# The last feed-forward product of a transformer encoder layer, turned so that tokens lie on the partitions

## The chip, the cores and the metric

The kernel runs on one core of a Trainium2 chip. The metric is the device time in microseconds of one execution of the whole program. Times before: 2081.9, 2083.98 and 2084.88 us in three runs, median 2083.98.

## The reference

Two sequences (`x_prompt`, `x_sample`) of 512 tokens and 1024 channels go through one encoder layer, each by itself, in float32. Only the end matters here:

```python
def rms_norm(x, g):
    y = x * lax.rsqrt(jnp.mean(x * x, axis=-1, keepdims=True) + EPS)
    return y * g

def swiglu(x, w_gate, w_up, w_down):          # D_FF = 2816
    return (silu(x @ w_gate) * (x @ w_up)) @ w_down

# end of the layer, for each sequence:
x = x + 0.5 * swiglu(rms_norm(x, ffn2_norm), ffn2_w_gate, ffn2_w_up, ffn2_w_down)
return rms_norm(x, final_norm)
```

Ahead of it lie a first feed-forward of the same form, attention and an mLSTM memory, which the change doesn't touch.

## The kernel before

Every float32 product is made from three passes: each operand is split into a high and a low part, and high x high, high x low and low x high are summed in PSUM.

**The second feed-forward's down product.** The two sequences and the two halves of the channels form a 2 x 2 block product, which is computed by the seven products of a Strassen scheme (named B11, B21, T2, T3, T4, T1, B22 in the order `DOWN`) and not by eight. `ffn_down` runs over 28 steps (`n_steps`): four chunks of the inner dimension (`CHUNKS`; the last is 8, 9, 10, three units each), and the seven products in each. In a step, `products` takes four blocks of 128 channels (`d`, `DH` = 4); in each block nine matmuls (three units, three passes) multiply 128x128 weights by 512 tokens into one PSUM bank: channels lie on the partitions, tokens along the row. Products T1 and B22 share a bank: B22 goes on accumulating where T1 stopped. Banks come from pools: `MM` (3 buffers, tile `mm`), `PO` (1, `pso`), `PS` (2, `pss`), `PT` (2, `pst`).

`flush_` (L597) evicts each bank on VectorE as `acc = 0.5 * psum + acc` into `xs[0]`, `xs[1]`, `e16` or `e5`. `xs[s]` holds sequence s of the layer's output with channels on the partitions: slots 0 to 3 the lower 512 channels, 4 to 7 the upper. In the last chunk it calls `done` as parts are final: sequence 0 after B21 (lower) and T4 (upper), the upper half of sequence 1 after T1, its lower half after B22, the very last step. That last step runs in two halves of 256 tokens (`halves`), so its matmuls have 256 columns.

**The final norm.** The sum over channels is needed for each token, and the output has tokens on its rows, so the results are turned by TensorE: `turn_out` (L1407) transposes four 128x128 blocks, one group of 128 tokens by 512 channels, into one `PS` or `PT` bank.

- `finish0` (sequence 0): sums of squares were collected in `acc0` during the flushes; `col_sums` (L200) transposes and reduces them, `stats` and `rsqrt_cols` (L165) compute 1/rms by an integer trick and three Newton steps, all on VectorE; then eight times transposes, one VectorE pass (`put_out`, L1420: times 1/rms times `final_norm`) and one transfer.
- `finish1_upper` (after T1): transposes of the upper half of sequence 1, a square with a row sum on ScalarE (`square`, L1435), and a multiply by `final_norm` on VectorE (L1442).
- `finish1(th)` (after each half of the last step): transposes of the lower half for two groups of 128 tokens, squares with sums in two pieces, 1/rms for both groups by `rsqrt_cols` in columns, then for each group two passes and two transfers.

All output transfers are issued from the SP queue, in order.

**The order of the work.** Each engine runs its instructions in a fixed order. A planner sets it: every instruction has a priority, by its place in the program, and an engine takes the ready one of lowest number. `shifted(n)` adds n to the numbers of a block; `LATER` = 100, used for `finish0`, sets it back by 100 instructions. So transposes of `finish0` and `finish1_upper` stand among the matmuls of the last step.

Of the kernel before, what the change touches and what calls it, by code (L numbers as in the profile page):

```python
# [16 lines left out]
P = 128  # L17
S = 512
D = 1024
KD = D // P  # L20
DFF = 2816
NF = DFF // P
EPS = 1e-6
# [3 lines left out]
def encoder(ctx, tc, I, outs):  # L27
    nc = tc.nc
# [106 lines left out]
    def A(shape, dtype=F32, name="a"):  # L135
        return apool.tile(shape, dtype, tag="a", name=nm(name))

    xs = [None, None]

    def xhl_tiles():  # L140
        return A([P, KD, S], F32R, "xh"), A([P, KD, S], F32R, "xl")
# [54 lines left out]
    def stats(acc):  # L196

        return rstd_cols(col_sums(acc), 4, D)

    def col_sums(acc, bs=(0, 1, 2, 3)):  # L200
        p = PT()
        for b in bs:
            nc.tensor.transpose(p[:, b * P:(b + 1) * P], acc[:, b * P:(b + 1) * P], ident)
        c = spool.tile([P, len(bs)], F32, tag=f"cs{len(bs)}", bufs=4, name=nm("cs"))
        nc.vector.tensor_reduce(c, p[:, bs[0] * P:(bs[-1] + 1) * P].rearrange("p (b d) -> p b d", d=P), axis=AX.X,
                                op=ALU.add)
        return c
# [294 lines left out]
    DH = KD // 2  # L502
    n_steps = len(DOWN) * len(CHUNKS)

    def ffn_down(wd, rb, ring, tail, xres, done, at_step, hook, halves=None):
        n = n_steps
        rt = [A([P, 4, 2, S], F32R, "rt") for _ in range(3)]
        e16 = A([P, KD, S], F32, "e16")
        xs[0], xs[1] = A([P, KD, S], F32, "xs"), A([P, KD, S], F32, "xs")
        e5 = A([P, DH, S], F32, "e5")  # L510
        right = [[t[:, q] for q in range(3)] for t in rt] + [[t[:, 3] for t in rt]]
# [65 lines left out]
        def products(i, ts, ds=range(DH)):  # L577
            m = DOWN[i % 7]
            first = m in (B11, T2_, T1)
            grp = "Y" if m in (T2_, T3, T4) else "X"  # L580
            for d in ds:
                if first:
                    banks[grp, d] = (((PS, PS, PT, PT) if grp == "Y" else (MM, MM, MM, PO))[d])()
                p = banks[grp, d][:, ts]
                us = left[i]
                for q, u in enumerate(us):
                    r = right[(i + 3) % 4][q]
                    for k, (a, b) in enumerate(((0, 0), (0, 1), (1, 0))):
                        nc.tensor.matmul(p, u[:, a, d * P:(d + 1) * P], r[:, b, ts],  # L589
                                         start=(first and q == 0 and k == 0), stop=(q == len(us) - 1 and k == 2),  # L590
                                         skip_group_check=True)
                flush_(i, d, p, ts)

        def add(t, u):
            V_.tensor_tensor(t, t, u, op=ALU.add)

        def flush_(i, d, p, ts):  # L597
            m, last = DOWN[i % 7], i >= n - 7
            acc = {B11: e16[:, d], T2_: e16[:, DH + d], T1: e5[:, d], B21: xs[0][:, d], T4: xs[0][:, DH + d],
                   T3: xs[1][:, DH + d], B22: xs[1][:, d]}[m]  # L600
            if last and m == T1:
                acc = xs[1][:, DH + d]
            if i < 7 and m in (B11, T2_, T1):
                nc.scalar.activation(acc, p, AF.Copy, scale=0.5)
            else:
                V_.scalar_tensor_tensor(acc[:, ts], p, 0.5, acc[:, ts], op0=ALU.mult, op1=ALU.add)
            if not last:
                return
            if m == B11:
                add(xs[0][:, DH + d], acc)  # L610
                add(xs[1][:, DH + d], acc)
                add(xs[1][:, d], acc)
            elif m == T2_:
                add(xs[1][:, d], acc)
            elif m == B21:
                add(xs[1][:, DH + d], e5[:, d])
                done(0, d, None)
            elif m == T4:
                done(0, DH + d, None)
            elif m == T1:  # L620
                done(1, DH + d, None)
            elif m == B22 and ts.stop - ts.start == S:
                done(1, d, None)
            elif m == B22 and d == DH - 1:
                done(1, d, ts.start * 2 // S)

        refill()
        for i in range(4):
# [6 lines left out]
        sums(CHUNKS[0])  # L635
        tail()
        for i in range(n):
            if i == n - 1 and halves:
                products(i, slice(0, S // 2))
                products(i, slice(S // 2, S))  # L640
            else:
                products(i, whole)
            prep(i + 2)
            load_right(i + 4)
            if i == 1:
                free.extend((1, *h4[k:k + 2]) for k in (0, 2))
                refill()
            if i == at_step:
                hook()
# [15 lines left out]
    def small(w, tag):  # L665
        return spool.tile([P, w], F32, tag=tag, bufs=2 if tag != "asm" else 6, name=nm(tag))
# [740 lines left out]
    def turn_out(s, b, half, p, ks=range(4)):  # L1407
        for k in ks:
            nc.tensor.transpose(p[:, k * P:(k + 1) * P], xs[s][:, half * 4 + k, b * P:(b + 1) * P], ident)
        return p  # L1410

    def put_out(s, b, half, p, r):

        o = T2()
        if s and half and b == 0:
            V_.tensor_scalar(o, p, r, None, op0=ALU.mult)
        elif s and half:
            nc.scalar.activation(o, p, AF.Copy, scale=r)
        else:
            V_.scalar_tensor_tensor(o, p, r, fn[half], op0=ALU.mult, op1=ALU.mult)  # L1420
        nc.sync.dma_start(outs[s][0, b * P:(b + 1) * P, half * S:(half + 1) * S], o)
# [9 lines left out]
    upper = []  # L1431

    def square(i, b, p):
        w = p.shape[-1]
        nc.scalar.activation(T2(F32, "f2")[:, 0:w], p, AF.Square, scale=D ** -0.5, accum_out=sq1[:, i, b:b + 1])  # L1435

    def finish1_upper():
        for b in range(4):
            p = turn_out(1, b, 1, (PS, PT)[b % 2]())
            square(0, b, p)  # L1440
            t = T2()
            V_.tensor_tensor(t, p, fn[1], op=ALU.mult)  # L1442
            upper.append(t)

    def finish1(th):
        bs = slice(2 * th, 2 * th + 2)
        cut = 2 * P
        ps_ = PS(), PT()
        for ks in (0, 1), (2, 3):
            for i in range(2):  # L1450
                turn_out(1, 2 * th + i, 0, ps_[i], ks)
                if ks[0] == 0:
                    square(1, 2 * th + i, ps_[i][:, 0:cut])
        sm, a = small(2, "fs2"), small(2, "fs2")
        V_.scalar_tensor_tensor(sm, sq1[:, 0, bs], EPS, sq1[:, 1, bs], op0=ALU.add, op1=ALU.add)
        for i in range(2):
            square(2, 2 * th + i, ps_[i][:, cut:S])
        V_.tensor_tensor(a, sm, sq1[:, 2, bs], op=ALU.add)
        r = rsqrt_cols(a, 2)
        with shifted(0 if th else LATER):  # L1460
            for j in range(4):
                i, half = j % 2, 1 - j // 2
                b = 2 * th + i
                put_out(1, b, half, upper[b] if half else ps_[i], r[:, i:i + 1])

    def done2(s, d, th):
        if s == 0:
            acc0[0] = sq_add(xs[0][:, d, :], acc0[0], "R", eng=V_ if d >= DH else None)
            if d == KD - 1:
                with shifted(LATER):  # L1470
                    finish0()
        elif d == KD - 1:
            finish1_upper()
        elif th is not None:
            finish1(th)

    ffn_down(I["ffn2_w_down"][0], rbuf[1], up.ring, tail, x2buf, done2, n_steps - 7, load_fn, halves=True)


def host_consts():  # L1480
# [39 lines left out]
```

## Time and profile before

| | |
|---|---|
| median of three runs | 2083.98 us (2081.9 to 2084.88) |
| the profiled execution | 2082.11 us |
| its span | 2080.3 us |
| granted TensorE clock | 0.997 of full speed |
| instructions | 27215 |
| busy: PE, PEld, DVE, ACT, POOL | 99%, 81%, 75%, 43%, 5% of the span |
| DMA | 454.33 MB moved, mean 218 GB/s |

The span runs from the first to the last event of the profiled execution; 1.8 us lie around it. PE is TensorE's matmuls (transposes too), PEld its weight loads, which overlap them, DVE VectorE, ACT ScalarE, POOL GpSimd, SP the engine that issues most transfers. A row of the timeline has the start in us, the duration, the engine, the line of the kernel, the operation, the tile written and those read, the shapes, and in brackets how long the engine idled before it and for whom. A row of a group has a count, the busy time in us, the mean of one in ns, and the idle time before. The mean duration of a matmul contains its way through the array, which overlaps the next one: its cost to TensorE is the pitch in the chain.

### The profile page before, as it was taken

The numbers are of one execution on the slowest core, as the hardware profiler recorded it, in microseconds if no ns is written. First come the engines' busy times: TensorE is split into PE (matmuls) and PEld (weight loads), VectorE is DVE, ScalarE is ACT, GpSimd is POOL, SyncE is SP. The second block draws the span as 40 slices with busy tenths as digits, with TensorE's granted clock in tenths as the row PEclk, the third lists the DMA queues.
The fourth block names the chain that finished last, engine by engine and source line by source line (L and its number), as shares of the span: only waits on it lengthen the run. The fifth ranks groups of instructions, "written<-read, shape, count | busy, mean of one in ns | idle before, by whom it ended". The sixth has DMA issues, their size and how long they took to land.

```text
span 2080.3 us, 27215 instructions
## 1 busy us (share of the span) xinstructions
PE 2060.4 (99%) x9478; PEld 1691.4 (81%) x9478; DVE 1551.1 (75%) x2836; ACT 894.6 (43%) x1645; POOL 97.7 (5%) x114
## 2 busy tenths in 40 slices
PE   8999999999999999999999999999999999999998
PEld 6888888888888877888878788888888888888887
DVE  7888888786797897575567646555788888786797
ACT  6544444443234566463345443324444444442222
POOL 1000000001003000100120000002000000000000
PEclk9999999999999999999999999999999999999999
DMA  9655655599766655777684345677656555599753
GB/s 280 203 173 194 193 171 182 200 342 362 262 222 243 218 152 174 265 240 268 210 286 160 107 149 190 208 255 245 200 177 200 192 172 182 187 348 347 270 189 116
DMA packets 307065, 454.33 MB, mean 218 GB/s; under 512 B 20064, under 2 KB 178864, under 8 KB 305904
## 3 DMA queue, kind: packets, MB, share of 16 engines
q1 hardware_dynamic: 305056, 447.13, 63.6%
q0 software_dynamic: 1872, 5.46, 0.8%
q8 instruction: 75, 1.23, 0.2%
q14 instruction: 62, 0.51, 0.1%
HBM read 285.63 MB, written 166.89 MB: 218 GB/s over the span
## 4 chain that ended last, share of the span: by engine, by line
PE 95%; DVE 3%; DMA 1%; ACT 1%; issue 0%; SPq 0%; DVEq 0%; ACTq 0%
PE mm L755 20%; PE pss L333 17%; PE pst L333 11%; PE mm L333 10%; PE mm L589 9%; PE pst L589 4%; PE pss L589 4%; PE mm L739 4%; PE pso L589 3%; PE pso L1029 1%; PE pss L1002 1%; PE pso L739 1%; PE pst L1021 1%; PE pso L1165 1%; PE pst L755 1%; PE pss L755 1%
## 5 line engine op out<-in xcount | busy, mean ns | idle before, releaser
L755 PE MATMUL mm<-xh,w 128*128 128x512 f32 x896 | 290.4, 394 | 0.0
L333 PE MATMUL pss<-xc,w 128*128 128x512 f32 x1056 | 256.2, 391 | 0.6 <-DVE t L364 0.6
L333 PE MATMUL mm<-xc,w 128*128 128x512 f32 x1056 | 253.4, 391 | 2.0 <-DVE w L292 0.7
L333 PE MATMUL pst<-xc,w 128*128 128x512 f32 x1056 | 253.6, 389 | 0.0
L333 PEld LDWEIGHTS pss<-xc,w 128*128 128x128 f32 x1056 | 196.9, 188 | 47.8 <-DVE t L364 7.2
L333 PEld LDWEIGHTS mm<-xc,w 128*128 128x128 f32 x1056 | 197.3, 188 | 45.2 <-DVE w L292 1.4
L333 PEld LDWEIGHTS pst<-xc,w 128*128 128x128 f32 x1056 | 198.2, 188 | 41.2
L755 PEld LDWEIGHTS mm<-xh,w 128*128 128x128 f32 x896 | 167.7, 188 | 33.5
L589 PE MATMUL mm<-rt,w 128*128 128x512 f32 (+1 forms) x819 | 188.4, 384 | 0.0
L755 PE MATMUL mm<-xl,w 128*128 128x512 f32 x448 | 176.2, 393 | 0.0
L589 PEld LDWEIGHTS mm<-rt,w 128*128 128x128 f32 x819 | 151.3, 188 | 29.8
L291 ACT ACTIVATE w<-t 128x512 fp32r<-128x512 f32 x176 | 106.9, 627 | 139.0 <-issue 55.2
L292 DVE TENSOR_TENSOR w<-t,w 128x512 fp32r<-128x512 f32 x176 | 118.3, 689 | 54.9 <-ACT w L291 52.9
L333 PE MATMUL pss<-xc,f 128*128 128x512 f32 x528 | 126.8, 389 | 0.0
L333 PEld LDWEIGHTS pss<-xc,f 128*128 128x128 f32 x528 | 99.1, 188 | 20.6
L657 ACT ACTIVATE w<-wr 128x512 fp32r<-128x512 f32 x72 | 45.1, 632 | 138.2 <-PE pso L589 70.8
L657 ACT ACTIVATE w<-t 128x512 fp32r<-128x512 f32 x82 | 51.8, 632 | 107.4 <-PE pst L589 62.4
L755 PEld LDWEIGHTS mm<-xl,w 128*128 128x128 f32 x448 | 84.2, 188 | 16.6
L589 PE MATMUL pss<-rt,w 128*128 128x512 f32 x396 | 93.7, 389 | 0.0
L589 PE MATMUL pst<-rt,w 128*128 128x512 f32 x396 | 93.7, 389 | 0.0
L239 ACT ACTIVATE w<-wr 128x1024 fp32r<-128x1024 f32 (+1 forms) x56 | 57.3, 1028 | 73.7 <-PE mm L755 30.2
L589 PEld LDWEIGHTS pss<-rt,w 128*128 128x128 f32 x396 | 74.3, 188 | 15.4
(343 smaller groups left out, 3641.6 us busy)
## 6 DMA issues: line engine op xcount, KB each, us to landing
rt<-rbuf SPq DMA_DIRECT2D x154, 512.0 KB, 5.4
wpark<-w SPq DMA_DIRECT2D x104, 512.0 KB, 3.4
w<-wpark SPq DMA_DIRECT2D x104, 512.0 KB, 4.7
wr<-in_ffn_w_gate_dram SPq DMA_DIRECT2D x62, 512.0 KB, 5.3
rbuf<-tab SPq DMA_DIRECT2D x102, 256.0 KB, 4.0
wr<-in_ffn_w_up_dram SPq DMA_DIRECT2D x44, 512.0 KB, 4.6
rbuf<-f SPq DMA_DIRECT2D x72, 256.0 KB, 4.0
wr<-in_w_in_dram SPq DMA_DIRECT2D x36, 512.0 KB, 6.0
```

What stands on the lines that cost most here:

```text
L239: pin(nc.scalar.activation(hi, raw, AF.Copy))
L291: pin(nc.scalar.activation(t[:, 0], src, AF.Copy))
L292: pin(V_.tensor_tensor(t[:, 1], src, f(t[:, 0]), op=ALU.subtract))
L333: nc.tensor.matmul(p, a[:, k, :], xt[:, b, k, :], start=(first and k == 0 and i == 0), stop=(k == HK_ - 1 and i == 2), skip_group_check=True)
L589: nc.tensor.matmul(p, u[:, a, d * P:(d + 1) * P], r[:, b, ts], start=(first and q == 0 and k == 0), stop=(q == len(us) - 1 and k == 2), sk ...
L657: nc.scalar.activation(hi, src, AF.Copy)
L739: nc.tensor.matmul(p[b][:, :N], a[:, k, bs], w_[:, kl, :], start=(k == 0 and i == 0), stop=(k == KD - 1 and i == 2))
L755: nc.tensor.matmul(p, a[:, k, :], b, start=(k == 0 and i == 0), stop=(k == n - 1 and i == 2))
L1002: nc.tensor.matmul(p, qT[:, h, b * P:(b + 1) * P], kv[:, hk * 2 + j, :], start=(j == 0), stop=(j == 1))
L1021: nc.tensor.transpose(p[:, b * P:(b + 1) * P], Ps[b][:, kb * P:(kb + 1) * P], ident)
L1029: nc.tensor.matmul(po, Vst[:, kv_, hk, :], w, start=(kv_ == 0 and i == 0), stop=(kv_ == 3 and i == 1))
L1165: nc.tensor.matmul(po, vm[:, a, t, hs_], b, start=(t == 0 and n == 0), stop=(t == 3 and n == 2))
```

## The change

- The last step (B22 of the last chunk) is computed turned, by `products_turned`: the 128x128 operand is now the tokens' side, the 512-column one the weights', so the product comes out with tokens on the partitions. It runs over four groups of 128 tokens; the last group in two halves of 256 columns. It no longer accumulates onto T1's banks, so T1 is added to the lower half of sequence 1 by an eviction of its own (four more VectorE passes in `flush_`).
- `turn1`, after T1, transposes both halves of sequence 1, without that last product, into the tile that was `e16` (now also `xs[2]`): the lower half by a ScalarE copy, the upper by a square with sum on ScalarE and a multiply by `final_norm` on VectorE.
- `finish1` handles each group as its product is there: add to the copy, square with sum, square root on ScalarE with the rest of the sum as its bias, reciprocal on VectorE, one pass for each half, two transfers. The upper half of the last group is issued from ScalarE's queue; its pass runs on ScalarE, except for group 2, where it runs on VectorE.
- `finish0` gets 1/rms by square root and reciprocal; of its eight output passes four stay on VectorE, and four become a ScalarE copy with scale and a GpSimd multiply.

```diff
-    xs = [None, None]
+    xs = [None, None, None]
...
-        e16 = A([P, KD, S], F32, "e16")
+        e16 = xs[2] = A([P, KD, S], F32, "e16")
...
+        def products_turned(i):
+            us = left[i]
+            for b in range(4):
+                cuts = (0, S) if b < 3 else (0, S // 2, S)
+                for j, c in enumerate(zip(cuts, cuts[1:])):
+                    cs = slice(*c)
+                    p = (MM, MM, MM, PO)[b - j]()
+                    for q, u in enumerate(us):
+                        r = right[(i + 3) % 4][q]
+                        for k, (a, h) in enumerate(((0, 0), (0, 1), (1, 0))):
+                            nc.tensor.matmul(p[:, cs], r[:, h, b * P:(b + 1) * P], u[:, a, cs],
+                                             start=(q == 0 and k == 0),
+                                             stop=(q == len(us) - 1 and k == 2), skip_group_check=True)
+                    turned(b, j, len(cuts) - 2 - j, p[:, cs], cs)
...
             elif m == T1:
+                if turned:
+                    V_.scalar_tensor_tensor(xs[1][:, d], p, 0.5, xs[1][:, d], op0=ALU.mult, op1=ALU.add)
                 done(1, DH + d, None)
...
-            if i == n - 1 and halves:
-                products(i, slice(0, S // 2))
-                products(i, slice(S // 2, S))
+            if i == n - 1 and turned:
+                products_turned(i)
...
+    eps = small(1, "eps")
+    nc.vector.memset(eps, EPS)
 
     def finish0():
-        r = stats(acc0[0])
+        c = col_sums(acc0[0])
+        r = small(4, "fs4")
+        nc.scalar.activation(r, c, AF.Sqrt, scale=1.0 / D, bias=eps)
+        V_.reciprocal(r, r)
         for j in range(8):
             b, half = j % 4, j // 4
-            put_out(0, b, half, turn_out(0, b, half, (PS, PT)[b % 2]()), r[:, b:b + 1])
+            p = turn_out(0, b, half, (PS, PT)[b % 2]())
+            o = T2()
+            if j % 2:
+                V_.scalar_tensor_tensor(o, p, r[:, b:b + 1], fn[half], op0=ALU.mult, op1=ALU.mult)
+            else:
+                nc.scalar.activation(o, p, AF.Copy, scale=r[:, b:b + 1])
+                G_.tensor_tensor(o, o, fn[half], op=ALU.mult)
+            nc.sync.dma_start(outs[0][0, b * P:(b + 1) * P, half * S:(half + 1) * S], o)
...
+    def turn1():
         for b in range(4):
+            p = turn_out(1, b, 0, (PS, PT)[b % 2]())
+            lo, up_ = xs[2][:, b], xs[2][:, DH + b]
+            nc.scalar.activation(lo, p, AF.Copy)
             p = turn_out(1, b, 1, (PS, PT)[b % 2]())
             square(0, b, p)
+            V_.tensor_tensor(up_, p, fn[1], op=ALU.mult)
+            rows1.append((lo, up_))
+            V_.tensor_scalar(sq1[:, 0, b:b + 1], sq1[:, 0, b:b + 1], EPS, None, op0=ALU.add)
...
+    def finish1(b, j, left, p, cs):
+        lo, up_ = rows1[b]
+        V_.scalar_tensor_tensor(lo[:, cs], p, 0.5, lo[:, cs], op0=ALU.mult, op1=ALU.add)
+        square(1 + j, b, lo[:, cs])
+        s0, s1 = sq1[:, 0, b:b + 1], sq1[:, 1 + j, b:b + 1]
+        if left:
+            V_.tensor_tensor(s0, s0, s1, op=ALU.add)
+            return
+        r = small(1, "fs1")
+        nc.scalar.activation(r, s1, AF.Sqrt, bias=s0)
+        V_.reciprocal(r, r)
+        if b == 2:
+            V_.tensor_scalar(up_, up_, r, None, op0=ALU.mult)
+        else:
+            nc.scalar.activation(up_, up_, AF.Copy, scale=r)
+        V_.scalar_tensor_tensor(lo, lo, r, fn[0], op0=ALU.mult, op1=ALU.mult)
+        for half, (t, q) in enumerate(((lo, nc.sync), (up_, nc.scalar if b == 3 else nc.sync))):
+            q.dma_start(outs[1][0, b * P:(b + 1) * P, half * S:(half + 1) * S], t)
```

More of the change, by code (lines that the diff above doesn't have):

```diff
@@ L503, in encoder, with ffn_down @@
     n_steps = len(DOWN) * len(CHUNKS)
-    def ffn_down(wd, rb, ring, tail, xres, done, at_step, hook, halves=None):
+    def ffn_down(wd, rb, ring, tail, xres, done, at_step, hook, turned=None):
         n = n_steps
         rt = [A([P, 4, 2, S], F32R, "rt") for _ in range(3)]
-        e16 = A([P, KD, S], F32, "e16")
+        e16 = xs[2] = A([P, KD, S], F32, "e16")
         xs[0], xs[1] = A([P, KD, S], F32, "xs"), A([P, KD, S], F32, "xs")
@@ L620, in flush_ @@
             elif m == T1:
+                if turned:
+                    V_.scalar_tensor_tensor(xs[1][:, d], p, 0.5, xs[1][:, d], op0=ALU.mult, op1=ALU.add)
                 done(1, DH + d, None)
-            elif m == B22 and ts.stop - ts.start == S:
+            elif m == B22:
                 done(1, d, None)
-            elif m == B22 and d == DH - 1:
-                done(1, d, ts.start * 2 // S)
         refill()
@@ L1410, in turn_out @@
         return p
[L1412 to L1421, printed above, removed]
+    eps = small(1, "eps")
+    nc.vector.memset(eps, EPS)
     def finish0():
-        r = stats(acc0[0])
+        c = col_sums(acc0[0])
+        r = small(4, "fs4")
+        nc.scalar.activation(r, c, AF.Sqrt, scale=1.0 / D, bias=eps)
+        V_.reciprocal(r, r)
         for j in range(8):
             b, half = j % 4, j // 4
-            put_out(0, b, half, turn_out(0, b, half, (PS, PT)[b % 2]()), r[:, b:b + 1])
+            p = turn_out(0, b, half, (PS, PT)[b % 2]())
[6 more added lines that the diff above has]
+            nc.sync.dma_start(outs[0][0, b * P:(b + 1) * P, half * S:(half + 1) * S], o)
     sq1 = spool.tile([P, 3, 4], F32, tag="sq8", bufs=1, name="sq1")
-    upper = []
+    rows1 = []
     def square(i, b, p):
@@ L1435, in square @@
         nc.scalar.activation(T2(F32, "f2")[:, 0:w], p, AF.Square, scale=D ** -0.5, accum_out=sq1[:, i, b:b + 1])
-    def finish1_upper():
+    def turn1():
         for b in range(4):
+            p = turn_out(1, b, 0, (PS, PT)[b % 2]())
+            lo, up_ = xs[2][:, b], xs[2][:, DH + b]
+            nc.scalar.activation(lo, p, AF.Copy)
             p = turn_out(1, b, 1, (PS, PT)[b % 2]())
             square(0, b, p)
-            t = T2()
-            V_.tensor_tensor(t, p, fn[1], op=ALU.mult)
-            upper.append(t)
@@ L1445, in finish1 @@
[L1445 to L1464, printed above, removed]
+            V_.tensor_tensor(up_, p, fn[1], op=ALU.mult)
@@ L1472, in done2 @@
         elif d == KD - 1:
[L1473 to L1477, printed above, removed]
+            turn1()
+    ffn_down(I["ffn2_w_down"][0], rbuf[1], up.ring, tail, x2buf, done2, n_steps - 7, load_fn, turned=finish1)
 def host_consts():
```

## The prediction

> **What bounds the kernel now.** I read the page first, then busy time by stretches of the end, then the chain, and last the timeline of each engine over the last 35 us, since the diff touches nothing earlier.
>
> ```profile
> span 2080.3 us, 27215 instructions
> PE 2060.4 (99%) x9478; PEld 1691.4 (81%) x9478; DVE 1551.1 (75%) x2836; ACT 894.6 (43%) x1645; POOL 97.7 (5%) x114
> ```
>
> TensorE is busy for 99% of the span, so only two things at the end can shrink: the time TensorE idles in the last step, and the time from its last instruction to the end. In the stretches below (columns: length, then busy time of PE, PEld, DVE, ACT, POOL, the granted clock, the DMA share and GB/s) the first is the T1 product of the last chunk, the second the last product among the transposes, the third the finish, the fourth only transfers.
>
> ```profile
> 2045.50:2054.20 8.70, 8.70 (x42) 7.07 (x41) 5.05 (x11) 0.63 (x1) 0.00 (x0) 1.00 0.01 2
> 2054.20:2070.10 15.90, 15.27 (x132) 15.02 (x131) 13.74 (x44) 4.37 (x16) 0.00 (x0) 1.00 0.36 133
> 2070.10:2076.10 6.00, 1.16 (x8) 0.52 (x6) 5.83 (x27) 3.51 (x11) 0.00 (x0) 0.78 0.47 175
> 2076.10:2080.30 4.20, 0.00 (x0) 0.00 (x0) 0.00 (x0) 0.00 (x0) 0.00 (x0) 0.50 0.66 249
> ```
>
> So 10.2 us pass after the last product, six of them in arithmetic with VectorE busy throughout. TensorE's timeline and the chain (start, time, what) give the pitch of its instructions and its two pauses:
>
> ```profile
> 2054.22 0.60 PE L1409 MATMUL pss<-ident,xs 128*128 128x128 f32 x4
> 2056.25 0.96 PE L589 MATMUL mm<-rt,w 128*128 128x256 f32 x6
> 2057.84 0.66 PE L1409 MATMUL pss<-ident,xs 128*128 128x128 f32 x4 [0.63 <-DVE t L1420]
> 2068.78 1.24 PE L589 MATMUL pso<-rt,w 128*128 128x256 f32 x9
> ...
> 2045.73 6.12 PE mm L589 x27
> 2061.17 0.44 PE pss L1409 x4
> 2067.15 1.79 PE mm L589 x15
> 2071.30 0.38 PE pst L1409 x2
> ```
>
> A 512-column product is 6.12/27 = 0.227 us, a 256-column one 1.79/15 = 0.119, a transpose 0.44/4 = 0.11. The work after T1 by groups (count behind the x):
>
> ```profile
> L589 PE MATMUL mm<-rt,w 128*128 128x256 f32 x54 | 9.6, 313 | 0.0
> L1409 PE MATMUL pst<-ident,xs 128*128 128x128 f32 x32 | 6.3, 275 | 0.0
> L1409 PE MATMUL pss<-ident,xs 128*128 128x128 f32 x32 | 5.8, 276 | 1.0 <-DVE t L1420 0.6 <-ACT f L1435 0.4
> L589 PE MATMUL pso<-rt,w 128*128 128x256 f32 x18 | 3.0, 292 | 0.0
> ```
>
> That is 64 transposes and 72 narrow products: 7.04 + 8.57 = 15.61 us from 2054.22, so 2069.83 without a pause; it ended at 2071.30 + 0.38 = 2071.68. About 0.9 of the 1.85 lost lies ahead of 2057.84, where a transpose waits for a bank that the first output pass of sequence 0 still holds; the rest lies in the last transposes, which wait for the squares.
>
> **Part 1, TensorE.** The transposes stay 64: 32 for sequence 0, 16 upper and 16 lower of sequence 1. The 16 lower ones move ahead of the last product, since they now turn the sums without it. The product becomes 27 wide and 18 narrow instructions: 6.12 + 2.14 = 8.26. From 2054.22 that makes 15.30, so the last product ends at 2069.5 if nothing pauses, and nothing on TensorE follows it.
>
> **Part 2, the tail.** The rows of the tail before, and of the transfers:
>
> ```profile
> 2070.34 0.42 DVE L606 SCALAR_TENSOR_TENSOR xs<-pso,xs 128x256 f32<-128x256 f32 x1
> 2072.03 0.39 ACT L1435 ACTIVATE f<-pst 128x256 f32<-128x256 f32 x1
> 2072.30 0.22 ACT L1435 ACTIVATION_READ_ACCUMULATOR f<-pst 128x1 f32 x1
> 2070.74 0.48 DVE L1416 TENSOR_SCALAR t<-t,rs 128x512 f32<-128x512 f32 x1
> 2072.55 0.16 DVE L1458 TENSOR_TENSOR fs<-fs,sq 128x2 f32<-128x2 f32 x1
> 2074.33 0.28 DVE L184 SCALAR_TENSOR_TENSOR rs<-rs,rs 128x1 f32<-128x1 f32 x2
> 2075.26 0.74 DVE L1420 SCALAR_TENSOR_TENSOR t<-pst,rs,t 128x512 f32<-128x512 f32 x1
> ...
> L1418 ACT ACTIVATE t<-t,rs 128x512 f32<-128x512 f32 x3 | 2.1, 716 | 2.0 <-DVE rs L184 2.0
> L1435 ACT ACTIVATE f<-pss 128x512 f32<-128x512 f32 x2 | 1.2, 600 | 14.6 <-PE pss L1409 14.6
> L816 ACT ACTIVATE gt<-mm,rs 128x16 f32<-128x16 f32 x6 | 1.8, 294 | 0.0
> L1421 SPq DMA_DIRECT2D out_dram<-t x16: 332/333/413, 2057.8 to 2076.8; - x16
> DMA to landing us min/median/max: 2.0/2.1/2.6
> ```
>
> Before: transposes, squares, then 2.1 us of small VectorE steps for 1/rms (2072.55 to 2074.61), two passes a token group, and four output transfers that leave one behind the other, the last issued at 2076.8, though its data was ready at 2075.26 + 0.74 = 2076.00. The span ends 3.5 after that issue.
>
> After, for the last 256 columns of the last 128 tokens, with 0.04 for each change of engine (the read ends at 2072.52, VectorE starts at 2072.55): the eviction waits about 0.1 for the last product and runs from 2069.6 to 2070.02; square and read take 0.49, to 2070.55; the square root has no row, and I price it by the nearest small ACTIVATE with a column operand, 0.29, to 2070.88; the reciprocal as a small step of 0.16, to 2071.08; the last multiply 0.74, to 2071.86, with the upper half's 0.72 on ScalarE beside it; both transfers leave at 2071.9 from two queues, behind no other. That is 2076.8 - 2071.9 = 4.9 us earlier.
>
> Against it stand three costs:
> The row of tokens before (b = 2) is in VectorE's queue. Its product ends 18 x 0.119 = 2.14 us before the end, at 2067.4; eviction 0.7, square 0.8, root 0.3 and reciprocal 0.2 bring it to 2069.5, just ahead of the last eviction. Its two remaining passes are 0.48 and 0.74. If they stand ahead of the last eviction, as program order has them, that starts 2069.5 + 1.22 = 2070.7 and not at 2069.6: 1.1 us; if the queue has them behind, 0. I take 0.7, nearer to program order.
> The pause of TensorE while sequence 0 waits for its 1/rms: between 0 and the 0.9 seen now. I take 0.3 (part 3).
> The first transfer ever issued from ScalarE's queue, and two at once: issues here take 0.33 to 0.41 and landings 2.0 to 2.6, so between 0 and 0.7. I take 0.1, because four queued ones drained before.
> Sum: 4.9 - 0.7 - 0.3 - 0.1 = 3.8 us less.
>
> **Part 3, 1/rms of sequence 0.**
>
> ```profile
> 2053.03 0.69 DVE L205 TENSOR_REDUCE cs<-pst 128x4 f32<-128x512 f32 x1 [0.45 <-PE pst L203]
> 2054.45 0.68 DVE L606 SCALAR_TENSOR_TENSOR xs<-pso,xs 128x512 f32<-128x512 f32 x1
> 2057.03 0.75 DVE L1420 SCALAR_TENSOR_TENSOR t<-pss,rs,t 128x512 f32<-128x512 f32 x1 [0.45 <-DVE rs L192]
> ...
> 673.12 1.28 ACT L875 ACT_TABLE_LOAD   x1
> 674.42 0.23 ACT L875 ACTIVATE fa<-fa 128x32 f32<-128x32 f32 x1
> ...
> L132 ACT ACT_TABLE_LOAD x1 | 1.3, 1283 | 0.7 <-PEq L1508 0.7
> L348 ACT ACT_TABLE_LOAD x1 | 1.3, 1283 | 2.4 <-issue 2.4
> ```
>
> The sums are there at 2053.72 and the first output pass starts at 2057.03, 3.3 later. After, Sqrt is a new function for ScalarE, so I count one table load. The one at L348 had 2.4 of idling before it, so I take a load as standing behind the wait of its ACTIVATE: 1.30 from load to ACTIVATE (673.12 to 674.42) and the root's 0.29 reach 2055.3. The reciprocal queues on VectorE behind the evictions of T1's last column, now two of 0.68 from 2054.45, so it is done near 2056.0, and the first output pass starts 1.0 earlier than 2057.03. With the passes split between VectorE and ScalarE two banks come free in the time of one, so the pause mostly closes. The Trainium skill (ScalarE: Activation LUTs, What ACT_TABLE_LOAD costs) puts a switch at 1283 ns and a drain of 1380 ns; by that the first pass would start near 2056.9, the pause would stay near 0.8 and the sum would be 3.3. This trace agrees on the 1283 and shows no drain between load and ACTIVATE.
>
> T1 now evicts each column block twice: 4 more VectorE passes of 0.68, three of them under T1's own products (VectorE is busy 5.05 of 8.70 there), the fourth under the transposes of sequence 0. POOL gets four multiplies:
>
> ```profile
> 2020.00 1.30 POOL L156 TENSOR_TENSOR R<-R,f 128x512 f32<-128x512 f32 x1 [1.10 <-ACT f L155]
> 2020.35 1.49 DVE L595 TENSOR_TENSOR xs<-xs,e 128x512 f32<-128x512 f32 x1
> ```
>
> They take 1.3 each, 5.2 in all, done near 2062, and the SP queue holds the later sequence 0 outputs until then; nothing of sequence 1 leaves before about 2062. A VectorE pass that reads two SBUF tiles beside one can stretch to 1.49; in that window only the first `lo` multiply does. Cost on the path 0, and 0.8 if that cover fails.
>
> **The rivals.**
> Clean tail: VectorE takes the last eviction ahead of row b = 2's passes, and no pause remains: 4.9 less, 2079.1. For it: the root may arrive late enough that the eviction is ready first. Against: program order.
> ScalarE paces the banks: from 2053.7 it now carries a load and root (1.6), four passes of sequence 0 (2.8), four copies and squares at 0.6 (4.8), and of rows 0 to 2 three squares with read (0.8), three roots (0.3) and two upper passes (0.72), 4.7: together 13.9 of the 15.8 us to TensorE's end. If the transposes of sequence 1 wait for its copies, uncovered by the 27 wide products, the pause is the load, the root and the 1.3 by which its copies and squares exceed their transposes' 3.5: 2.9 in place of 0.3, so the gain is 1.2, and the time 2082.8. For it: 4.37 busy becomes 13.9. Against: the products of rows 0 to 2 need only banks that T1 has left, so they can cover.
> The other side: Sqrt and Square in different tables. Then each row pays two loads, about nine more of 1.28, 11.5 us on ScalarE. With b = 3's own 1.3 the 13.9 becomes 26.7, to 2080.4; 1.0 to the last multiply's end and 3.5 to the end make 2084.9, so 4.6 more than the span now if ScalarE never idles, and I take 5: 2089. It decides from about the second extra load, as ScalarE has some 1.9 to spare. Against: the groups have table loads at L132, L348 and L875 to L877 alone (seven in all; first and last row above), none at a square or a copy, though these ran under other functions' tables. The Trainium skill (ScalarE: Activation LUTs, Table sets: the hidden batching unit) says that cheap functions such as copy are in every set; it does not name Square there, and no run here shows Sqrt.
>
> **How the numbers follow.** The profiled execution took 2082.11 (span 2080.3 and 1.8 around it); 3.8 less is 2078.3. The median of the runs is 1.87 higher, so on it 2083.98 - 3.8 = 2080.2. About 0.2% (4.2 us) is what a measurement of this kernel can tell from no change: the bounds are 2079.8 and 2088.1. Chances: forecast 0.48, clean tail 0.30, ScalarE paces 0.14, tables 0.08. The forecast lies so near the bound that I give 0.08 of its 0.48 to faster: faster 0.38, same 0.40 + 0.14 = 0.54, slower 0.08. The range runs from the clean tail less the 1.6 by which runs stray (2077.5) to ScalarE pacing plus 1.7 (2084.5); the table case stays outside.
>
> **What would show it.** Right: the last product ends near 2069.5 to 2070.2 with no transpose behind it, one table load near 2054, the last issue 2 to 3.5 us after the last product, from two queues. The DVE order around the last 128x256 eviction tells forecast from clean tail. Wrong: table loads between squares and roots, TensorE pauses beyond 1 us between 2054 and 2069 with ACT as the releaser, or a last transfer that lands much over 2.6 after its issue.

## The result, and the profile after

| | before | after |
|---|---|---|
| median of 22 runs each | 2082.82 us (2081.3 to 2084.88) | 2079.98 us (2078.24 to 2081.82) |
| the profiled execution, its span | 2082.11, 2080.3 us | 2079.39, 2077.5 us |
| ratio of the times | | 0.9986, 95% interval 0.9979 to 0.9992 |

The kernel became 2.8 us faster by the medians, 1.7 to 4.4 by the interval; 3.8 had been forecast. The gain is clear of noise, but below the 0.2% at which the prediction draws its line.

The page of the changed kernel:

```profile
span 2077.5 us, 27122 instructions
PE 2059.7 (99%) x9451; PEld 1689.1 (81%) x9451; DVE 1547.5 (74%) x2798; ACT 901.6 (43%) x1653; POOL 103.7 (5%) x118
```

Its busy time over the same stretches as before, columns as there:

```profile
2045.50:2054.20 8.70, 8.70 (x42) 7.12 (x41) 6.38 (x11) 2.50 (x4) 0.00 (x0) 1.00 0.01 2
2054.20:2070.10 15.90, 15.79 (x107) 13.57 (x106) 10.97 (x23) 10.72 (x25) 4.98 (x4) 1.00 0.44 165
2070.10:2076.10 6.00, 0.97 (x9) 0.77 (x7) 3.28 (x9) 2.99 (x10) 0.00 (x0) 1.00 0.70 262
2076.10:2077.50 1.40, 0.00 (x0) 0.00 (x0) 0.00 (x0) 0.00 (x0) 0.00 (x0) 0.57 0.00 0
```

In the second stretch TensorE is now busy for 15.79 of 15.90 us, and VectorE has given 2.8 us of its 13.74 away; ScalarE has gone from 4.37 to 10.72. In the third VectorE has 3.28 where it had 5.83. TensorE's timeline at the start and end of the last product:

```profile
2054.92 0.60 PE L1424 MATMUL pss<-ident,xs 128*128 128x128 f32 x4
2056.59 0.94 PE L605 MATMUL mm<-w,rt 128*128 128x512 f32 x3
2057.37 0.63 PE L1424 MATMUL pss<-ident,xs 128*128 128x128 f32 x4
2058.27 1.33 PE L1424 MATMUL pss<-ident,xs 128*128 128x128 f32 x8
2069.83 1.24 PE L605 MATMUL mm<-w,rt 128*128 128x256 f32 x9
```

The first transpose of sequence 0 starts at 2054.92, 0.70 later than before. Up to 2051.7 both traces have the same matmuls in the same order (9329 records), and TensorE is full. The traces are 0.9 us apart by 1106 us into the run and between 0.6 and 0.75 from 1317 on, far ahead of the change, so it is how two executions differ. I therefore use **the stage** from here: the time from that first transpose to the end of the span. It was 2080.34 - 2054.22 = 26.12, and is 2077.54 - 2054.92 = 22.62 us: 3.50 less. How well it repeats shows where an edit comes only behind the last product: in three such kernels below (GpSimd pass, SP's queue, output in halves) the last matmul starts at 15.87 to 15.90 of the stage, and here at 15.87.

The last product ends at 2069.83 + 9 x 0.119 = 2070.90. What follows on VectorE and ScalarE:

```profile
2071.11 0.42 DVE L1466 SCALAR_TENSOR_TENSOR e<-mm,e 128x256 f32<-128x256 f32 x1 [0.27 <-PE mm L605]
2071.57 0.42 ACT L1451 ACTIVATE f<-e 128x256 f32<-128x256 f32 x1
2071.89 0.19 ACT L1451 ACTIVATION_READ_ACCUMULATOR f<-e 128x1 f32 x1
2072.11 0.29 ACT L1473 ACTIVATE fs<-sq 128x1 f32<-128x1 f32 x1
2072.11 0.74 DVE L1479 SCALAR_TENSOR_TENSOR e<-e,fs,t 128x512 f32<-128x512 f32 x1
2072.78 0.15 DVE L1474 RECIPROCAL fs<-fs 128x1 f32<-128x1 f32 x1
2072.97 0.75 DVE L1479 SCALAR_TENSOR_TENSOR e<-e,fs,t 128x512 f32<-128x512 f32 x1
```

And sequence 1's output transfers by line (count, duration, first and last start):

```profile
L1481 SPq DMA_DIRECT2D out_dram<-e x7: 332/332/382, 2067.7 to 2073.7; - x7
L1481 ACTq DMA_DIRECT2D out_dram<-e x1: 396/396/396, 2073.7 to 2073.7; - x1
```

The chain of the prediction is there step by step. One place is late: the last group's root ends at 2072.40, and the reciprocal starts only at 2072.78, because VectorE is in the third group's lower pass (2072.11, 0.74). Both last transfers leave at 2073.7.

### The profile page after: what moved, and what is told of

Read it like the earlier page. It is cut to its first block, busy times and chain, and to the rows that moved or that the text cites. A ratio compares the mean times of both kernels' runs of the same rounds, so it can differ in the third digit from the quotient of the medians.

```text
span 2077.5 us, 27122 instructions
## 1 busy us (share of the span) xinstructions
PE 2059.7 (99%) x9451; PEld 1689.1 (81%) x9451; DVE 1547.5 (74%) x2798; ACT 901.6 (43%) x1653; POOL 103.7 (5%) x118
## 4 chain that ended last, share of the span: by engine, by line
PE 94%; DVE 2%; DMA 1%; ACT 1%; issue 0%; SPq 0%; ACTq 0%; DVEq 0%
PE mm L770 20%; PE pss L333 17%; PE pst L333 11%; PE mm L333 10%; PE mm L589 8%; PE pst L589 4%; PE pss L589 4%; PE mm L754 4%; PE pso L589 3%; PE pso L1044 1%; PE pss L1017 1%; PE pso L754 1%; PE pst L1036 1%; PE pso L1180 1%; PE pst L770 1%; PE pss L770 1%
## 5 line engine op out<-in xcount | busy, mean ns | idle before, releaser
L589 PE MATMUL mm<-rt,w 128*128 128x512 f32 x765 | 178.8, 389 | 0.0
L589 PEld LDWEIGHTS mm<-rt,w 128*128 128x128 f32 x765 | 143.5, 188 | 29.8
L589 PEld LDWEIGHTS pst<-rt,w 128*128 128x128 f32 x396 | 74.3, 188 | 15.4
```

## The experiments

The changed kernel has three separable parts: the turned product, the root in place of Newton steps, and sequence 0's passes split between VectorE and ScalarE with GpSimd. "Issue" is the start of the last output transfer within the stage. Each kernel was timed beside the kernel before; the ratios have intervals of about 0.1% to either side, too wide to tell most of these apart, so the verdicts rest on the stage, from one profile each. What the stage saves and what the ratio saves differ by 0.9 us at most over all kernels here, so they agree within the intervals. The eight kernels behind the table have ratios of 0.9982 to 0.9988, each clear of 1, none of them clear of the others.

| kernel | stage | issue | ratio to before (95%) |
|---|---|---|---|
| before | 26.12 | 22.58 | |
| after | 22.62 | 18.82 | 0.9986 (0.9979 to 0.9992) |
| root only | 23.96 | 20.42 | 0.9990 (0.9981 to 0.9999) |
| root and split, not turned | 23.85 | 20.28 | 0.9989 (0.9980 to 0.9999) |
| turned and split, Newton | 27.41 | 23.63 | 1.0004 (0.9995 to 1.0014) |
| turned and root, no split | 23.77 | 19.89 | 0.9989 (0.9980 to 0.9999) |

**The root alone.** In the kernel before:

```diff
-        r = stats(acc0[0])
+        c = col_sums(acc0[0])
+        r = small(4, "fs4")
+        nc.scalar.activation(r, c, AF.Sqrt, scale=1.0 / D, bias=eps)
+        V_.reciprocal(r, r)
...
-        r = rsqrt_cols(a, 2)
+        r = small(2, "fs2")
+        nc.scalar.activation(r, a, AF.Sqrt)
+        V_.reciprocal(r, r)
```

> The kernel before with 1/rms of both sequences by square root and reciprocal; the last product is not turned. Stage = from the first transpose of sequence 0's output to the end of the span: 26.1 us before, 22.6 after. Theory (two parts that add up, turning the larger): each last group of tokens loses about 1.4 us of VectorE steps (1.87 from the shift to the last Newton step, against about 0.5 for root and reciprocal), and the 0.9 us pause of TensorE in front of sequence 0's second bank mostly closes: stage 24.2 to 24.8. Rival (the root is the whole gain, turning gives back in four evictions and copies what it takes from the end): stage 22.6 to 23.0.

Stage 23.96: 2.16 less than before, more than the 1.3 to 1.9 of the theory and far from the rival. The pause of 0.9 ahead of the first bank is gone (the last transpose starts at 16.37 of the stage, not at 17.17), and at the end, on VectorE:

```profile
2073.10 0.17 DVE L1467 RECIPROCAL fs<-fs 128x2 f32<-128x2 f32 x1 [0.27 <-ACT fs L1466]
2073.38 0.75 DVE L1420 SCALAR_TENSOR_TENSOR t<-pss,fs,t 128x512 f32<-128x512 f32 x1
2074.05 0.74 DVE L1420 SCALAR_TENSOR_TENSOR t<-pst,fs,t 128x512 f32<-128x512 f32 x1
```

The last pass ends at 2074.79, 19.63 into the stage (from 2055.16), where it was 2076.00 - 2054.22 = 21.78: of the 2.15, 0.8 lies ahead of the last transpose, where the pause was, and 1.35 between it and the last pass, where the Newton steps of the last two groups stood.

**Turned, with Newton steps.** In the changed kernel `rstd_cols(c, 4, D)` for sequence 0, and for each group:

```diff
-        r = small(1, "fs1")
-        nc.scalar.activation(r, s1, AF.Sqrt, bias=s0)
-        V_.reciprocal(r, r)
+        s = small(1, "fs1")
+        V_.tensor_tensor(s, s0, s1, op=ALU.add)
+        r = rsqrt_cols(s, 1)
```

The small tiles of these steps also have six buffers here, not ten.

> The changed kernel with 1/rms of both sequences by the old Newton steps on VectorE, in columns of one. Theory (two parts that add up): the end of the last row gets one add and nine small steps in place of root and reciprocal, 1.4 to 2.0 us more, and the other rows' steps load VectorE with some 5 us more: stage 24.2 to 25.0. Rival (the root is the whole gain): stage about 26, no better than before.

Stage 27.41: both were too low. Without the root the turned kernel is 1.29 slower than before by the stage; the interval of its ratio holds 1 too. Busy time of this kernel over the first 10 us of the stage and from there to its last pass (DVE is the third busy time):

```profile
2055.93:2065.93 10.00, 9.72 (x72) 8.16 (x71) 6.65 (x19) 5.94 (x13) 4.97 (x4) 1.00 0.46 172
2065.93:2079.53 13.60, 6.51 (x40) 5.66 (x38) 12.59 (x55) 6.54 (x16) 0.00 (x0) 0.92 0.38 143
```

The same of the changed kernel:

```profile
2054.92:2064.92 10.00, 9.89 (x76) 8.54 (x75) 6.37 (x14) 7.06 (x16) 4.98 (x4) 1.00 0.56 211
2064.92:2073.72 8.80, 6.15 (x36) 5.28 (x34) 7.20 (x17) 6.64 (x19) 0.00 (x0) 1.00 0.39 147
```

VectorE has no more work than in the kernel before: 6.65 + 12.59 = 19.2 us, and 13.74 + 5.83 = 19.6 there in the two stretches of the prediction. But a third of the first 10 us it has nothing to do, as in the changed kernel, and the rest is packed behind, 12.59 of 13.60 us: it is the bound of the end. What the fewer buffers add was not tried; it can't be much more than the 1.0 us that VectorE idles there. The root takes 5.7 us of it away. VectorE's timeline shows how groups hinder each other in one queue; the third group's passes stand amid the last group's Newton steps:

```profile
2076.07 0.15 DVE L171 TENSOR_SCALAR rs<-fs 128x1 int32<-128x1 int32 x1
2076.19 0.48 DVE L1474 TENSOR_SCALAR e<-e,rs 128x512 f32<-128x512 f32 x1
2076.59 0.74 DVE L1477 SCALAR_TENSOR_TENSOR e<-e,rs,t 128x512 f32<-128x512 f32 x1
2077.25 0.15 DVE L173 TENSOR_SCALAR rs<-rs 128x1 int32<-128x1 int32 x1
...
2078.59 0.16 DVE L184 SCALAR_TENSOR_TENSOR rs<-rs,rs 128x1 f32<-128x1 f32 x1
2078.78 0.75 DVE L1477 SCALAR_TENSOR_TENSOR e<-e,rs,t 128x512 f32<-128x512 f32 x1
```

TensorE's last matmul starts only 0.36 later than in the changed kernel (16.23 against 15.87 of the stage), so nearly all of the 4.79 (27.41 - 22.62) lies behind the products.

**All of the change but the turned product.** The root-only kernel with sequence 0's passes split as the change splits them (`if j % 2:` VectorE, else ScalarE and GpSimd).

> The kernel before with the root and with sequence 0's passes split between VectorE and ScalarE with GpSimd: all of the change but the turned product. So far the stage is 26.1 before, 24.0 with the root alone, 22.6 with all, 23.8 with all but the split, 27.4 with all but the root. Theory (the split pays only where the rows of the turned product need VectorE; without them the end is a chain of two groups behind the last product): stage 23.6 to 24.0, turning worth 1.0 to 1.4 of the 3.5. Rival (the split is worth its 1.15 here too): stage 22.7 to 23.0, and turning next to nothing.

Stage 23.85, as the theory had it: unturned, the split is worth 0.11. So turning gives 23.85 - 22.62 = 1.23 on top of the other two, while turning and the split without the root made the kernel 1.29 slower than before (the split alone, with Newton steps, was not run). The parts do not add.

**All of the change but the split.**

```diff
-            if j % 2:
+            if True:
                 V_.scalar_tensor_tensor(o, p, r[:, b:b + 1], fn[half], op0=ALU.mult, op1=ALU.mult)
```

> The changed kernel with all eight output passes of sequence 0 on VectorE, none on ScalarE and GpSimd. Theory (TensorE's pause of 0.7 us between the transposes comes from how fast banks are let go, and two engines let go faster than one): the pause grows to 1.0 to 1.6, stage 22.9 to 23.5. Rival (ScalarE paces the banks, with 10.7 of 15.9 us busy): taking its four passes away closes the pause, stage 21.9 to 22.1.

Stage 23.77, 1.15 more, but not by the theory's way: the last product comes at the same place (15.85 against 15.87). The 3 us more on VectorE came out at the end, behind the products, as in the Newton run: the last issue is 1.07 later, and VectorE is busy for 8.63 us behind the first 10 of the stage, in place of 7.20. So the split pays where the turned rows need VectorE, and hardly elsewhere.

**The third group's upper pass on GpSimd.**

```diff
         if b == 2:
-            V_.tensor_scalar(up_, up_, r, None, op0=ALU.mult)
+            G_.tensor_scalar(up_, up_, r, None, op0=ALU.mult)
```

> The changed kernel with the upper pass of the third group of tokens on GpSimd and not on VectorE. Theory (VectorE's queue holds up the last row: the last reciprocal waited 0.38 us behind the third group's lower pass): that pass begins 0.4 earlier, the reciprocal follows the root within 0.06, stage 22.2 to 22.4. Rival (the end is set by the output transfers of the third and fourth group, which follow each other on the DMA engines with hardly a break): the last transfers are issued earlier but land no earlier, stage 22.6.

Stage 23.60, outside both. On the engines:

```profile
2073.04 2.10 POOL L1476 TENSOR_SCALAR e<-e,fs 128x512 f32<-128x512 f32 x1 [9.45 <-DVE sq L1470]
2073.35 0.29 ACT L1473 ACTIVATE fs<-sq 128x1 f32<-128x1 f32 x1
2073.68 0.16 DVE L1474 RECIPROCAL fs<-fs 128x1 f32<-128x1 f32 x1
2073.88 0.92 DVE L1479 SCALAR_TENSOR_TENSOR e<-e,fs,t 128x512 f32<-128x512 f32 x1
2074.63 0.37 ACTq L1481 DMA_DIRECT2D out_dram<-e  x1
```

VectorE's part is as the theory said: the reciprocal follows the root at once, and ScalarE's transfer leaves at 18.47 of the stage in place of 18.79. But the GpSimd pass took 2.10 us, and its transfer stands in SP's queue ahead of two others whose data were ready; they left up to 19.93. The wait went from one in-order queue to another.

**The last upper half from SP's queue** (`nc.scalar if b == 3 else nc.sync` becomes `nc.sync`).

> The changed kernel with the last upper half issued from SP's queue, behind the last lower half's neighbour, and none from ScalarE's. In the changed kernel the last two issues stand 18.79 and 18.82 us into the stage, and the span ends 3.8 after them, where it was 3.5 before. Theory (the 0.28 is the data of two transfers at once, 1.36 us on the DMA engines in place of the rest of one): the second issue comes some 0.45 later, but its data still waits for the first's, so the stage stays 22.6 to 22.75. Rival (ScalarE's queue costs the 0.28): the last issue 0.45 later and the end 3.5 behind it, the first transfer out of the way, so the issue sets the end: stage 22.75 to 23.0 with 3.5 from the last issue to the end.

Stage 22.59, the last issue at 19.27: 0.45 later, and the end where it was, 3.3 behind it. The theory holds: in both kernels the DMA engines are full from 19.7 to 21.1 of the stage (a share of 0.96 and 0.98, some 0.37 MB a us: two transfers of 256 KB), so the data follow one another, and ScalarE's queue neither costs nor gains.

**The last group in one piece** (`cuts = (0, S)` for all groups).

> The changed kernel with the last group of tokens in one piece of 512 columns, not in two halves. Theory (what stands behind the last product is a chain whose length goes by its width): product 0.1 shorter, eviction 0.27 and square 0.22 longer: stage 22.9 to 23.1. Rival (the queues of VectorE and ScalarE at the end are full, and four instructions fewer free them): stage 22.3 to 22.6.

Stage 22.72, between the two. Its last matmul starts 0.21 earlier, and the last issue comes 0.10 later. Halving buys 0.1, not 0.4.

**The gain ahead of the root.**

```diff
         square(1 + j, b, lo[:, cs])
+        V_.tensor_tensor(g[:, cs], lo[:, cs], fn[0][:, cs], op=ALU.mult)
...
-        V_.scalar_tensor_tensor(lo, lo, r, fn[0], op0=ALU.mult, op1=ALU.mult)
+        V_.tensor_scalar(g, g, r, None, op0=ALU.mult)
...
```

Here `g` is a new tile for each group, and the lower transfer takes its data from it.

> The changed kernel with the lower pass of each group cut in two: the multiply by final_norm into another tile directly behind the eviction, while ScalarE squares and takes the root, and behind the reciprocal only a multiply by a column, 0.48 in place of 0.75. Theory (the end is a chain on which a pass behind the root counts and one beside it doesn't): the last pass 0.27 shorter, the third group's 0.27 to 0.35 shorter ahead of the last reciprocal: stage 22.0 to 22.2. Rival (VectorE is full, as with the eight passes there that cost 1.15 for 3 us): the four multiplies more, 2.9 us on VectorE, cost about as much: stage 23.0 to 23.6.

Stage 22.76, 0.14 worse. The last pass is 0.49, as meant, but the third group's passes and an extra multiply stand in VectorE's queue ahead of the small add whose sum the last root takes as its bias:

```profile
2071.99 0.48 DVE L1480 TENSOR_SCALAR e<-e,fs 128x512 f32<-128x512 f32 x1
2072.39 0.48 DVE L1483 TENSOR_SCALAR t<-t,fs 128x512 f32<-128x512 f32 x1
2072.78 0.42 DVE L1471 TENSOR_TENSOR t<-e,t 128x256 f32<-128x256 f32 x1
2073.12 0.15 DVE L1474 TENSOR_TENSOR sq<-sq 128x1 f32<-128x1 f32 x1
2073.37 0.29 ACT L1477 ACTIVATE fs<-sq 128x1 f32<-128x1 f32 x1 [0.74 <-DVE sq L1474]
```

The root waits 0.74 for it. Neither size was right; the rival's reason, a full VectorE, is the one that shows.

**Two copies on VectorE, and the transposes spread.** Two edits at TensorE's pause: the lower copies of the first two groups by `V_.tensor_copy`; and `turn1` for the third and fourth group called at the end of `finish1` of the first and second.

> The changed kernel with the lower copies of the first two groups of tokens on VectorE, not on ScalarE. In the changed kernel TensorE lost 0.7 us between 2057 and 2062, each time waiting for a bank that ScalarE let go, while VectorE idled for 2.6 us. Theory (ScalarE paces the banks there): the pause closes to 0.2 to 0.4, stage 22.1 to 22.4. Rival (the pause belongs to the order in which the transposes stand on TensorE, or VectorE's in-order queue puts the copies late): pause 0.6 or more, stage 22.5 to 23.

> The changed kernel with the transposes of the third and fourth group of sequence 1, their copies, squares and multiplies, placed in the program behind the products of the first and second group, not all ahead of the products. So far TensorE lost 0.6 to 0.7 us among the transposes, whether ScalarE, VectorE or both let the banks go. Theory (transposes stand closer together on TensorE than four banks can be let go, so wide products between them close the pause): last product 0.4 to 0.6 earlier, stage 22.0 to 22.3. Rival (the copies and squares that move later meet the rows' own squares on ScalarE and hold up the end): last product earlier, but stage 22.7 or more.

Stages 22.59 and 23.24; the last product starts its last matmul at 15.83 and 15.86. Neither moved the pause, and both stages are where the rivals had them. What TensorE's weight loads waited for between 2054 and 2073, the longest row each (total, times, longest wait), without the split:

```profile
PEld pst L1424 <- ACT e L1457: 0.3, 1, 0.3
```

with the copies moved:

```profile
PEld pss L1424 <- ACT t L1442: 0.5, 2, 0.3
```

and spread:

```profile
PEld pst L1424 <- ACT e L1457: 0.4, 1, 0.4
```

In these rows the releaser is a ScalarE pass, and which one changes with the edit; VectorE passes have 0.5 us beside it without the split, 0.3 with the copies moved. That ScalarE paces the banks as a whole isn't shown, since taking four passes from it did not help. Spreading made the stage 0.62 longer, though not by the rival's way: the last squares are done on ScalarE by 2071.89, but the last root waits for the small add, which VectorE runs only behind the third group's passes:

```profile
2071.78 0.75 DVE L1479 SCALAR_TENSOR_TENSOR e<-e,fs,t 128x512 f32<-128x512 f32 x1
2072.44 0.15 DVE L1470 TENSOR_TENSOR sq<-sq 128x1 f32<-128x1 f32 x1
2072.69 0.29 ACT L1473 ACTIVATE fs<-sq 128x1 f32<-128x1 f32 x1 [0.81 <-DVE sq L1470]
```

**The table load behind the wait.** One more line ahead of sequence 0's root: `nc.scalar.activation(warm, c[:, 0:1], AF.Silu)`.

> The changed kernel with a Silu of one column of sequence 0's sums ahead of the square root: Silu's table is the one in place, so the table load for the root now stands behind the wait for the sums and is no longer covered by ScalarE's idle time (5.4 us, the load at 2048.2). Theory (the load takes 1.28 us and nothing else, and 1/rms of sequence 0 is nearly covered by other work of TensorE): 0.2 for the Silu and 1.3 for load to root in the chain of sequence 0, the pause ahead of the first bank 0.6 to 1.4 more, stage 22.9 to 24.0. Rival (a drain belongs to a switch): 2.7 from load to root, stage 24 or more. Second rival (1/rms of sequence 0 is off the path): stage 22.6.

```profile
2054.57 0.20 ACT L1433 ACTIVATE warm<-cs 128x1 f32<-128x1 f32 x1 [6.47 <-DVE cs L205]
2054.78 1.28 ACT L1434 ACT_TABLE_LOAD   x1
2056.08 0.30 ACT L1434 ACTIVATE fs<-cs,eps 128x4 f32<-128x4 f32 x1
```

From load to root 1.30, no drain. The root starts 1.3 later in the stage than in the changed kernel, but the stage is 22.83, only 0.21 more: between the theory, which was too high, and the second rival. The cover is VectorE's queue: without the edit the reciprocal waits for T1's evictions until 1.41 of the stage, with it until 1.60 for the root.

**The last output in halves.**

```diff
+        if b == 3:
+            for c in (slice(0, S // 2), slice(S // 2, S)):
+                V_.scalar_tensor_tensor(lo[:, c], lo[:, c], r, fn[0][:, c], op0=ALU.mult, op1=ALU.mult)
+                nc.sync.dma_start(outs[1][0, b * P:(b + 1) * P, c], lo[:, c])
+            nc.scalar.dma_start(outs[1][0, b * P:(b + 1) * P, S:2 * S], up_)
+            return
```

> The changed kernel with the last lower pass and its transfer in two halves of 256 columns, so that the first data can leave 0.33 us earlier. Theory (behind the last issue the two last transfers need the DMA engines for 1.36 us, so the end goes by when their first data starts): stage 22.2 to 22.4. Rival (a transfer's fixed time behind the last issue sets the end, and there is one issue more on SP's queue, 0.4 to 0.5 apart): stage 22.6 to 22.9.

Stage 22.42, just above the theory's range: the first half leaves at 18.56, the others at 18.79 and 18.98, and the end is 3.44 behind the last issue, in place of 3.80. It has the lowest stage of all; the median is 2079.22, ratio 0.9982 (0.9973 to 0.9992). Against the kernel before it is clear of 1; against the changed kernel the 0.2 us is one profile's, and the ratios can't tell it.

## Why the prediction was right, point by point

**TensorE.** The last product was put 15.3 behind the first transpose plus a pause of 0.3; it ended 15.98 behind it (2070.90 - 2054.92). The pause is 0.7, of which almost none stands where it was expected, at the first bank (2056.59 to 2057.37 holds three wide matmuls of 0.23 and 0.1 of waiting); it lies in 2058 to 2061, where for example eight transposes take 1.33, while 8 x 0.11 and the 0.16 that the last one needs to its end (0.60 for four) make 1.04. This term was mis-sized by 0.4. Three edits failed to close it, and why it stays is open.

**The tail.** From the end of the last product to the issue 2.4 was worked out without a hold, 3.1 with the 0.7 for VectorE's queue; it took 2073.72 - 2070.90 = 2.82. The third group's passes did hold up the last row's work, but not by the step that the forecast named. It had them ahead of the last eviction by program order; VectorE's queue has the last eviction first (2071.11, waiting for its product alone), and the third group behind it:

```profile
2070.93 0.28 ACT L1473 ACTIVATE fs<-sq 128x1 f32<-128x1 f32 x1
2071.45 0.15 DVE L1474 RECIPROCAL fs<-fs 128x1 f32<-128x1 f32 x1
2071.72 0.48 DVE L1476 TENSOR_SCALAR e<-e,fs 128x512 f32<-128x512 f32 x1
```

By the sign that the prediction gave, the order around the last eviction, the clean tail was right here. What the passes hold up is the last reciprocal, by 0.38, which neither had; the GpSimd run shows it go when the upper pass moves. That 0.38 lies between the 0 and the 1.1 from which 0.7 was taken is luck. Without the hold it is 2.44, as worked out.

**The transfers.** The end is 3.80 behind the last issue, before 3.54; 0.1 had been allowed. It is the data of two transfers and not ScalarE's queue: moving the issue to SP's queue changes nothing. The transfer from ScalarE's queue landed 2.7 after its issue, hardly more than the 2.6 seen before.

**The sum.** Issue earlier by 22.58 - 18.82 = 3.76, end later behind it by 0.26: 3.50 in the stage, against 3.8. The three misses partly cancel: 0.4 too little for the pause, 0.3 too much for the hold, 0.2 too little for the transfers. The medians show 2.84, and the interval, 1.7 to 4.4, holds the 3.50 and the 3.8. The time itself, 2080.2 forecast and 2079.98 measured, is closer than the working earns: the three runs before had a median 1.16 above that of all 22, and the gain by the medians was 0.96 smaller than forecast.

**1/rms of sequence 0.** One step of the prediction was wrong: the load does not stand behind the wait.

```profile
L1433 ACT ACT_TABLE_LOAD  x1: 1283/1283/1283, 2048.2 to 2048.2; - x1
...
2054.91 0.30 ACT L1433 ACTIVATE fs<-cs,eps 128x4 f32<-128x4 f32 x1 [5.39 <-DVE cs L205]
2056.33 0.17 DVE L1434 RECIPROCAL fs<-fs 128x4 f32<-128x4 f32 x1
```

It ran at 2048.2, in ScalarE's idle time, and the root started 0.04 after the sums (2054.18 + 0.69). The reciprocal then waited behind T1's two evictions, as predicted. It cost little to be wrong here: with the load put behind the wait the stage grows by 0.21. The Trainium skill (ScalarE: Activation LUTs, What ACT_TABLE_LOAD costs) has 1283 ns and a drain of 1380 for a switch. Both loads here take the 1.28; the one put behind the wait has its root 0.02 after it and shows no drain, and at 2048.2 a drain could hide in the idle time.

**The rivals.** The clean tail had the order on VectorE right and fell by the pause and the hold, 0.7 + 0.38, neither of which it had. ScalarE pacing: it is the releaser of 1.0 of the 1.2 us that the weight loads wait in the changed kernel, but its load was 10.7 and not 13.9 in the 15.9 us, and relieving it changed nothing. Tables: one load, at 2048.2, and none in the stage, where five Sqrts stand among nine squares and eleven copies.

**What the prediction did not see** is how the parts hang together. It priced the Newton steps as 2.1 us in the last groups' chain. The root alone is worth 2.16, but in the turned kernel 4.79, because there VectorE is the bound of the end; and the turned product, which gives the change its name, is worth 1.23 with the root and the split; without the root the whole is slower than before by the stage.

## What to carry to other kernels

When work at the end of a kernel is cut into pieces that each finish by themselves, look at the engine that all pieces share: here the turned kernel with Newton steps had no more VectorE work than the kernel before and yet ended 1.3 us later by the stage, with that engine full behind the products, and replacing the small steps by one on another engine was what made the cut pay. Measure the parts of such a change one by one and together, since they need not add, and from a common event in the trace when executions stray by more than the effect. A transfer or a pass that is moved to another engine also moves its place in an in-order queue: look at what stands behind it there.

## What the runs showed of the hardware that was not expected

GpSimd's multiply by a column, 128x512, took 2.10 us at the end of the run above, beside VectorE passes that read two SBUF tiles; eight of the same shape elsewhere in the kernel before have a mean of 0.96, which mixes two cases:

```profile
L938 POOL TENSOR_SCALAR box<-box,hn 128x512 f32<-128x512 f32 x8 | 7.7, 964 | 278.5 <-ACT box L937 278.5
```

Five of them take 0.68 to 0.69. The three that run beside a VectorE pass that reads two SBUF tiles (`w<-wr,w`) take 1.19, 1.42 and 1.66. The VectorE pass that ran beside the end of the 2.10 took 0.92 in place of 0.75; the one ahead of it, beside its start, took 0.74. And the start of the stage strayed between 2054.2 and 2057.9 over the profiles here, although no edit changes TensorE's work ahead of the last chunk's T1: a stray of 3.6 us, as large as the whole gain.
